# Two heads at a time on halves of the TensorE array in a hybrid attention layer

## Chip, cores and metric

One core of one Trainium2 chip runs the whole program. The metric is the device time of one execution in microseconds (us); the median of three runs is given. The engines are TensorE (PE; its weight loads are listed apart as PEld), VectorE (DVE), ScalarE (ACT), GpSimd (POOL) and SyncE (SP), which here issues every DMA.

## What is computed

Two layers over 512 frames of width 1024, all in float32. Each layer projects the normalised input, runs three groups of heads side by side (head width 64), projects their outputs back, and applies a squared-ReLU feed-forward of width 4096. Cut to what matters:

```python
z = rms(x, norm1) @ w_in
ya = swa(...)      # A: 8 query heads, 2 kv heads, window of whole 64-frame chunks, sinks
yb = fox(...)      # B: 4 heads, blocks of 128 queries
#   s = q @ k.T / 8 + F[q] - F[k]; causal; p = softmax(s); o = p @ v
yc = mlstm(...)    # C: 4 heads; scores Sm = (q @ k.T) * exp(Dm - m) per block, plus a running state
x = x + concat([ya, yb, yc]) @ w_out
x = x + square(relu(rms(x, norm2) @ w_ff1)) @ w_ff2
```

## The kernel before

Every large weight matmul is done as three matmuls on parts of float32 numbers (`mm3`, lines 306 to 308: high times high, high times low, low times high). ACT rounds a weight tile to its high part (line 201), DVE subtracts to get the low part (line 202). These weight matmuls are called W below; one over 512 columns in the output projection follows the next by about 0.23 us.

The attention stage of a layer interleaves W with the small matmuls of the three head groups. `fill(us)` puts W into the program until a credit of that many microseconds is used up; generators `runA`, `runB` and `runC` put small steps between. PE, DVE and ACT each work through their own queue in order; a scheduler has set that order when the program is built, mostly along the order of the code. `att()` hands out one of eight PSUM banks of 128x512.

A small float32 matmul is two matmul instructions in the trace (two passes), so counts in the profile are twice those of the code; the transposes through `ident` are one. Shapes such as `64*128` tell how many rows and columns of the 128x128 array the instruction uses: all small matmuls are full (`128*128`) except these:

- A, scores (line 763): `64*128`, the two kv heads `r` lie in the two row halves. Values (line 819): `128*64`, `r` picks the column half. A chunk from the third on has further keys, whose value product (line 822) is full and is added to the same bank.
- B, scores (line 864): `64*128`, head `2*pr + r` lies in row half `r`; a causal mask is added by a bf16 matmul (line 866, full). Values (line 900): `128*64`, into column half `r` of the bank `pobs[pr]`.
- C, scores (line 964): `64*128`.

In `runB` a unit is a head and a block `n` of 128 queries, 16 units a layer, with `nk = (n+1)*128` keys. Step s1 does the scores and the softmax: DVE adds the row of F and takes the maximum (line 869), negates it (871), ACT takes the exponential and its sum (873), DVE divides (875, 876). s2 transposes the probabilities (885) and copies them out of PSUM (888 on ACT, 890 on DVE). s3 multiplies by the values (900). `runC` makes a decay table E per head (line 951, from a row that a DMA spreads over the partitions, `rowb`), multiplies the scores into it (965), forms numerator and denominator (976 to 992), normalises (995 to 997), gates on POOL (1001), and transposes back (1008). The lines that close a layer's attention stage:

```python
        fill_to("wo0")     # output projection, inputs from A
        c_tail(0)          # transposes of heads 0, 1 of C
        fill(3.0, "wo1")   # output projection, inputs from B (yg tiles 4 and 5)
        c_tail(1)          # transposes of heads 2, 3 of C
        fill_to("wo1")
```

Of the kernel before, what the change touches and what calls it, by code (L numbers as in the profile page):

```python
# [25 lines left out]
NT = S // P  # L26
NCH = S // 64
# [18 lines left out]
def trunk(ctx, tc, x, cols, rows, gate_w, tabs, w_in, w_out, w1, w2, out):  # L46
    nc = tc.nc
    V, A, G, T = nc.vector, nc.scalar, nc.gpsimd, nc.tensor
# [11 lines left out]
    def nm(s):  # L60
        cnt[0] += 1
        return f"{s}_{cnt[0]}"

    ATT = {"ms": (S, 5), "zq": (640, 6), "zv": (260, 8), "tmp": (768, 3), "rowb": (S, 2),
           "qk": (2 * S, 5), "pT": (S, 4), "hs": (256, 2), "co": (256, 4)}
    FFP = {"xbx": (8 * D, 1), "fraw": (S, 9), "fs": (S, 6), "ct": (S, 6), "ms": (S, 2)}
    phase = {}
# [242 lines left out]
    ident = cst.tile([P, P], F32, name="ident")  # L310
# [97 lines left out]
    identb = cst.tile([P, P], BF16, name="identb")  # L408
    trib = cst.tile([P, P], BF16, name="trib")
# [29 lines left out]
    def rowb(drow, r):  # L439
        b = wt("rowb", "rowb")  # L440
        nc.sync.dma_start(b, drow[r:r + 1, :].broadcast_to((P, S)))
        return b
# [29 lines left out]
            rope.append((Cg, Sg))  # L472
        LPS[l].update(sk=sk, onorm=onorm, gb=gb, rope=rope)

    FA, FB = 1.4, 0.21
    F0, F1, F2 = 0, 4.5, 1.5
    FG = 4
    for l in range(L):
# [25 lines left out]
        gate = {}  # L504
# [43 lines left out]
        done = set()  # L548
# [199 lines left out]
        def runA():  # L748
# [5 lines left out]
            st = {}  # L754
# [57 lines left out]
            def s3(c):  # L812
                t, odd = divmod(c, 2)
                w, vt, p1, p2 = st.pop(c)
                po = att()
                for g in range(2):
                    for r in range(2):
                        u = 2 * g + r
                        T.matmul(po[r * 64:(r + 1) * 64, g * P:(g + 1) * P], vt[:w, r * 64:(r + 1) * 64],  # L819
                                 p1[:w, u * P:(u + 1) * P], start=True, stop=p2 is None)  # L820
                    if p2 is not None:
                        T.matmul(po[:, g * P:(g + 1) * P], vbd[:, c % 4], p2[:, g * P:(g + 1) * P],  # L822
                                 start=False, stop=True)
                cols = slice(c * 64, (c + 1) * 64)
                A.activation(yg[:, 0:4, cols], v3(po[:, :256]), AF.Copy)
                V.tensor_tensor(yg[:, 8:12, cols], v3(po[:, :256]), yg[:, 0:4, cols], ALU.subtract)

            for i in range(NCH + 2):
                if i < NCH:
                    s1(i)  # L830
                yield
                if 0 <= i - 1 < NCH:
                    s2(i - 1)
                yield
                if 0 <= i - 2 < NCH:
                    s3(i - 2)
                yield

        qTB, kTB, qTC, kTC = [None] * 4
# [11 lines left out]
                             scale=gfox(l, i))  # L851

        def runB(qTB, kTB):
            units = [(h, n) for h in range(4) for n in range(NT)]
            st, pobs, fbs = {}, {}, {}

            def s1(u):
                h, n = units[u]
                pr, r = divmod(h, 2)
                if n == 0:  # L860
                    fbs[h] = rowb(gate["drow"], h)
                nk = (n + 1) * P
                sp = att()
                T.matmul(sp[:, :nk], qTB[r * 64:(r + 1) * 64, pr, n * P:(n + 1) * P],  # L864
                         kTB[r * 64:(r + 1) * 64, pr, :nk], start=True, stop=False)
                T.matmul(sp[:, n * P:nk], identb, trib, start=False, stop=True)  # L866
                scs = wt("ms", "scs")
                mx = smt(1, "mxb")
                V.tensor_tensor_reduce(scs[:, :nk], sp[:, :nk], fbs[h][:, :nk], 1.0, -3.0e38, ALU.add, ALU.max, mx)
                nmx = smt(1, "nmxb")  # L870
                V.tensor_scalar(nmx, mx, -1.0, None, ALU.mult)
                ssum = smt(1, "ssb")
                A.activation(scs[:, :nk], scs[:, :nk], AF.Exp, bias=nmx, accum_out=ssum)
                rec = smt(1, "recb")
                V.reciprocal(rec, ssum)
                V.tensor_scalar(scs[:, :nk], scs[:, :nk], rec, None, ALU.mult)
                st[u] = scs

            def s2(u):
                h, n = units[u]  # L880
                nk = (n + 1) * P
                scs = st.pop(u)
                pt = att()
                for b in range(n + 1):
                    T.transpose(pt[:, b * P:(b + 1) * P], scs[:, b * P:(b + 1) * P], ident)  # L885
                p_ = wt("pT", "pTb")
                if n % 2:
                    A.activation(p_[:, :nk], pt[:, :nk], AF.Copy)
                else:
                    V.tensor_copy(p_[:, :nk], pt[:, :nk])  # L890
                st[u] = p_

            def s3(u):
                h, n = units[u]
                pr, r = divmod(h, 2)
                if r == 0 and n == 0:
                    pobs[pr] = att()
                p_ = st.pop(u)
                for b in range(n + 1):
                    T.matmul(pobs[pr][r * 64:(r + 1) * 64, n * P:(n + 1) * P], zbv[b][:, h * 64:(h + 1) * 64],  # L900
                             p_[:, b * P:(b + 1) * P], start=b == 0, stop=b == n)
                if r == 1 and n == NT - 1:
                    A.activation(yhi(4 + pr), pobs[pr], AF.Copy)
                    V.tensor_tensor(ylo(4 + pr), pobs[pr], yhi(4 + pr), ALU.subtract)

            for i in range(len(units) + 2):
                if i < len(units):
                    s1(i)
                yield
                if 0 <= i - 1 < len(units):  # L910
                    s2(i - 1)
                yield
                if 0 <= i - 2 < len(units):
                    s3(i - 2)
                yield

        def prepC(t, qTC, kTC):
# [23 lines left out]
        def runC(qTC, kTC, C):  # L941
# [13 lines left out]
                                fill=0.0, base=0, channel_multiplier=-1)  # L955
                es[h] = e

            def s1(h):
                pr, r = divmod(h, 2)
                rs = slice(r * 64, (r + 1) * 64)  # L960
                sp = att()
                for sb in range(NT):
                    cs_ = slice(sb * P, (sb + 1) * P)
                    T.matmul(sp[:, cs_], kTC[rs, pr, cs_], qTC[rs, pr, cs_], start=True, stop=True)  # L964
                V.tensor_tensor(es[h], sp, es[h], ALU.mult)
                yield

            def s2(h):
# [43 lines left out]
            def run():  # L1012
                for i in range(4 + 2):
                    if i < 4:
                        yield from s0(i)
                    yield
                    if 0 <= i - 1 < 4:
                        yield from s1(i - 1)
                    yield
                    if 0 <= i - 2 < 4:  # L1020
                        yield from s2(i - 2)
# [30 lines left out]
        for _ in runA():  # L1052
            fill(FA, "co")
            step += 1
            if step in (4, 7):
                next(g2_, None)
            if "bk" in done and step >= 9 and step % 2 == 0 and bt < 2 * NT:
# [6 lines left out]
        ct = 0  # L1064
        gb = runB(qTB, kTB)
        qTC, kTC = qk2("qTC"), qk2("kTC")
        cst_ = wt("qk", "state")[:, :780].rearrange("p (b r v) -> p b r v", b=3, r=2)
        G.memset(cst_, 0.0)
        for i in range(8):
            next(gb)  # L1070
# [9 lines left out]
        while live:  # L1080
            for g_ in list(live):
                if next(g_, "end") == "end":
                    live.remove(g_)
                fill(FB, "wo0")
        fill_to("wo0")
        c_tail(0)
        fill(3.0, "wo1")
# [216 lines left out]
```

## Time and profile before

| | |
|---|---|
| median of 3 runs | 1168.75 us (1167.68 to 1170.32) |
| span of the profiled execution, first to last instruction | 1168.6 us |
| PE busy | 1161.6 us, 99% |
| DVE busy | 856.5 us, 73% |
| ACT busy | 590.7 us, 51% |
| POOL busy | 60.8 us, 5% |
| granted TensorE clock, mean | 0.998 |

The page gives the span alone for the profiled execution; it lies 0.15 us below the median of the runs, so a sum against the span is a sum against the time. Layer 0's group A runs from 83.1 us (first line 763) to 156.1 us (first line 864), its groups B and C from there to 227.1 us (the second block of line 1008); layer 1's from 660 to 805 us in the same pattern. Matmuls overlap their neighbours in the trace, so that the distance from one start to the next tells what one costs, and not its listed duration.

### The profile page before, as it was taken

What the parts mean: (1) busy time and instruction counts of PE and PEld (TensorE: products, weight loads), DVE (VectorE), ACT (ScalarE), POOL (GpSimd) and SP (SyncE); (2) the same over time, 40 slices, a digit from 0 to 9 for tenths busy, and PEclk for the clock granted to TensorE, in tenths of its full rate; (3) what the DMA queues carried; (4) which work ended last, traced back from release to release, by engine and by line L of the source; (5) the groups of instructions that cost most, each with busy time, mean ns of one, the idle gap of its engine ahead of it and who ended that gap; (6) DMA issues with size and microseconds to landing.
All of it is one profiled execution on the core that took longest, in us unless ns stands there. A gap on an engine that the chain in (4) does not pass through costs nothing.

```text
span 1168.6 us, 19784 instructions
## 1 busy us (share of the span) xinstructions
PE 1161.6 (99%) x7348; PEld 1012.7 (87%) x7348; DVE 856.5 (73%) x1803; ACT 590.7 (51%) x1249; POOL 60.8 (5%) x98
## 2 busy tenths in 40 slices
PE   8999999999999999999999999999999999999998
PEld 8999877787899989889899988777788898998887
DVE  7686766798587687676867776777975776786684
ACT  5445654365454454455444465634645554554551
POOL 2020011103000000000001100110000000000000
PEclk9999999999999999999999999999999999999999
DMA  6332122243242332321333321214232233232221
GB/s 219 117 91 64 55 77 68 80 141 105 73 123 84 96 114 82 118 63 47 116 92 99 92 63 56 69 54 149 91 96 86 91 107 105 87 121 88 64 73 72
DMA packets 60000, 107.69 MB, mean 92 GB/s; under 512 B 7152, under 2 KB 8560, under 8 KB 59904
## 3 DMA queue, kind: packets, MB, share of 16 engines
q1 hardware_dynamic: 59904, 106.43, 29.5%
q8 instruction: 58, 0.95, 0.3%
q14 instruction: 38, 0.31, 0.1%
HBM read 103.82 MB, written 2.13 MB: 91 GB/s over the span
## 4 chain that ended last, share of the span: by engine, by line
PE 98%; DMA 1%; SPq 0%; DVE 0%; issue 0%; ACT 0%; ACTq 0%
PE at L306 29%; PE at L307 28%; PE at L308 28%; PE at L864 2%; PE at L900 2%; PE at L763 1%; PE at L819 1%; PE at L822 1%; PE at L885 1%; PE at L964 1%; PE at L796 1%; PE at L982 1%; DMA prm<-in_rows_dram 0%; DMA xT<-in_x_dram 0%; PE at L866 0%; DMA raw<-in_w_in_dram 0%
## 5 line engine op out<-in xcount | busy, mean ns | idle before, releaser
L201 ACT ACTIVATE whi<-raw 128x512 fp32r<-128x512 f32 x264 | 167.0, 633 | 217.8 <-PE at L307 155.2
L306 PE MATMUL at<-yg,whi 128*128 128x512 f32 (+1 forms) x644 | 255.5, 398 | 0.0
L307 PE MATMUL at<-yg,whi 128*128 128x512 f32 (+1 forms) x644 | 253.0, 393 | 0.0
L308 PE MATMUL at<-yg,wlo 128*128 128x512 f32 (+1 forms) x644 | 252.9, 393 | 0.0
L202 DVE TENSOR_TENSOR wlo<-raw,whi 128x512 fp32r<-128x512 f32 x264 | 180.2, 688 | 83.4 <-ACT whi L201 78.5
L306 PE MATMUL at<-whi,xh 128*128 128x256 f32 (+1 forms) x640 | 187.4, 293 | 1.3 <-ACT whi L201 1.3
L307 PE MATMUL at<-wlo,xh 128*128 128x256 f32 (+1 forms) x640 | 181.9, 284 | 0.1
L308 PE MATMUL at<-whi,xl 128*128 128x256 f32 (+1 forms) x640 | 181.8, 284 | 0.0
L308 PEld LDWEIGHTS at<-yg,wlo 128*128 128x128 f32 x644 | 121.0, 188 | 28.3
L306 PEld LDWEIGHTS at<-yg,whi 128*128 128x128 f32 x644 | 121.2, 188 | 24.0 <-issue 0.7
L307 PEld LDWEIGHTS at<-yg,whi 128*128 128x128 f32 x644 | 121.2, 188 | 24.1 <-issue 0.7
L306 PE MATMUL at<-xh,whi 128*128 128x256 f32 (+1 forms) x416 | 131.9, 317 | 0.0
L307 PE MATMUL at<-xl,whi 128*128 128x256 f32 (+1 forms) x416 | 131.3, 316 | 0.0
L308 PE MATMUL at<-xh,wlo 128*128 128x256 f32 (+1 forms) x416 | 131.1, 315 | 0.0
L306 PEld LDWEIGHTS at<-whi,xh 128*128 128x128 f32 x640 | 122.4, 191 | 5.5 <-issue 3.4
L307 PEld LDWEIGHTS at<-wlo,xh 128*128 128x128 f32 x640 | 122.2, 191 | 0.5 <-DVE wlo L202 0.4
L308 PEld LDWEIGHTS at<-whi,xl 128*128 128x128 f32 x640 | 122.3, 191 | 0.0
L201 ACT ACTIVATE whi<-fraw 128x512 fp32r<-128x512 f32 x96 | 60.8, 633 | 101.5 <-PE at L307 101.5
L307 PE MATMUL at<-xbx,whi 128*128 128x256 f32 x384 | 108.0, 281 | 0.0
L306 PE MATMUL at<-xbx,whi 128*128 128x256 f32 x384 | 107.9, 281 | 0.0
L308 PE MATMUL at<-xbx,wlo 128*128 128x256 f32 x384 | 107.8, 281 | 0.0
L202 DVE TENSOR_TENSOR wlo<-fraw,whi 128x512 fp32r<-128x512 f32 x96 | 65.0, 688 | 47.1 <-ACT whi L201 42.8
(268 smaller groups left out, 1931.9 us busy)
## 6 DMA issues: line engine op xcount, KB each, us to landing
raw<-in_w_dram SPq DMA_DIRECT2D x160, 256.0 KB, 2.6
fraw<-in_w_dram SPq DMA_DIRECT2D x96, 256.0 KB, 2.7
raw<-in_w_in_dram SPq DMA_DIRECT2D x80, 256.0 KB, 2.7
raw<-in_w_out_dram SPq DMA_DIRECT2D x32, 256.0 KB, 2.6
rowb<-drow SPq DMA_DIRECT2D x16, 256.0 KB, 3.4
xT<-in_x_dram SPq DMA_DIRECT2D x8, 256.0 KB, 4.5
out_dram<-xT SPq DMA_DIRECT2D x7, 256.0 KB, 2.1
cssn<-in_tabs_dram SPq DMA_DIRECT2D x2, 256.0 KB
```

What stands on the lines that cost most here:

```text
L201: A.activation(hi[:, :512], src, AF.Copy)
L202: V.tensor_tensor(lo[:, :512], src, hi[:, :512], ALU.subtract)
L306: T.matmul(o, sh, mh, start=first, stop=False)
L307: T.matmul(o, sh, ml, start=False, stop=False)
L308: T.matmul(o, sl, mh, start=False, stop=last)
L763: T.matmul(sc[r][:, g * 256:g * 256 + nk], qTA[g][r * 64:(r + 1) * 64, c * P:(c + 1) * P], kTA[r * 64:(r + 1) * 64, k0:k0 + nk], start=Tru ...
L796: T.transpose(pt[:w, u * P:(u + 1) * P], pe[:, u, :w], ident)
L819: T.matmul(po[r * 64:(r + 1) * 64, g * P:(g + 1) * P], vt[:w, r * 64:(r + 1) * 64], p1[:w, u * P:(u + 1) * P], start=True, stop=p2 is None)
L822: T.matmul(po[:, g * P:(g + 1) * P], vbd[:, c % 4], p2[:, g * P:(g + 1) * P], start=False, stop=True)
L864: T.matmul(sp[:, :nk], qTB[r * 64:(r + 1) * 64, pr, n * P:(n + 1) * P], kTB[r * 64:(r + 1) * 64, pr, :nk], start=True, stop=False)
L885: T.transpose(pt[:, b * P:(b + 1) * P], scs[:, b * P:(b + 1) * P], ident)
L900: T.matmul(pobs[pr][r * 64:(r + 1) * 64, n * P:(n + 1) * P], zbv[b][:, h * 64:(h + 1) * 64], p_[:, b * P:(b + 1) * P], start=b == 0, stop= ...
```

## The change

1. A's s3: the four value matmuls of a chunk stand together, then the two full ones; s3 stands right behind s1 of a later chunk, and a chunk has two `fill` steps and not three. `FA` goes from 1.4 to 2.1.
2. B: a unit is a pair of heads and a block, 8 units a layer. The scores of both heads stand next to each other, in the two row halves, then the two masks; the value matmuls alternate between the column halves. Negation and reciprocal are done once for both heads (128x2). Copies of the probabilities go to DVE for the even head and to ACT for the odd one. s3 follows s1. The scores have a buffer tag of their own (`scs`, 4), apart from `ms`; `rowb` has 4 buffers and not 2.
3. C: the scores of two heads alternate between the row halves, after the decay tables of both.
4. The steps of B, C and W are dealt out anew; `FB` goes from 0.21 to 0.33. 2 KB a partition are set aside for DMAs that software describes, which gives room for the buffers.

```diff
-    ATT = {"ms": (S, 5), ..., "rowb": (S, 2),
+    ATT = {"ms": (S, 5), ..., "rowb": (S, 4), "scs": (S, 4),
-    FA, FB = 1.4, 0.21
+    FA, FB = 2.1, 0.33
 # runA, s3
-                for g in range(2):
-                    for r in range(2):
-                        u = 2 * g + r
-                        T.matmul(po[r*64:(r+1)*64, g*P:(g+1)*P], vt[:w, ...], p1[:w, ...], start=True, stop=p2 is None)
-                    if p2 is not None:
-                        T.matmul(po[:, g*P:(g+1)*P], vbd[:, c % 4], p2[:, ...], start=False, stop=True)
+                for u in range(4):
+                    g, r = divmod(u, 2)
+                    T.matmul(po[r*64:(r+1)*64, g*P:(g+1)*P], vt[:w, ...], p1[:w, ...], start=g == 0, ...)
+                if p2 is not None:
+                    for g in range(2):
+                        T.matmul(po[:, g*P:(g+1)*P], vbd[:, c % 4], p2[:, ...], start=False, stop=True, ...)
 # runA and runB, the loop over units
                 s1(i)
+                s3(i - 2)
                 yield
                 s2(i - 1)
                 yield
-                s3(i - 2)
-                yield
 # runB
-            units = [(h, n) for h in range(4) for n in range(NT)]
+            units = [(pr, n) for pr in range(2) for n in range(NT)]
+                sps = [att(), att()]
+                for r, sp in enumerate(sps):
+                    T.matmul(sp[:, :nk], qTB[rs, pr, n*P:(n+1)*P], kTB[rs, pr, :nk], start=True, stop=False)
+                for sp in sps:
+                    T.matmul(sp[:, n*P:nk], identb, trib, start=False, stop=True)
...
+                for b in range(n + 1):
+                    for r in range(2):
+                        T.matmul(pobs[pr][r*64:(r+1)*64, n*P:(n+1)*P], zbv[b][:, ...], ps[r][:, b*P:(b+1)*P], ...)
 # runC, s1
-            def s1(h):
+            def s1(pr):
+                sps = [att(), att()]
                 for sb in range(NT):
-                    T.matmul(sp[:, cs_], kTC[rs, pr, cs_], qTC[rs, pr, cs_], start=True, stop=True)
+                    for r, sp in enumerate(sps):
+                        T.matmul(sp[:, cs_], kTC[rs, pr, cs_], qTC[rs, pr, cs_], start=True, stop=True)
 # driver of B and C
-        live = [gc, gb]
-        while live: ...
+        for _ in gc:
+            ct += 1
+            fill(FB, "wo0")
+            if 5 * bt < 2 * ct:
+                bt += 1
+                next(gb, None)
+                fill(FB, "wo0")
+        for _ in gb:
+            fill(FB, "wo0")
```

In the changed file the lines have moved: 819 is 818, 864 to 866 keep their numbers, 885 is 889, 900 is 906, 903 is 909, 964 is 969, 982 is 988, 1001 is 1007, 1008 is 1014.

How PE's queue stands at a chunk of group A, layer 0, before (`zar`, `vsh` and `kva` hold values, `pT` probabilities, `z` rows of B that are transposed):

```order
L848 MATMUL at_1687<-ident,z_848 128x128 x4
L819 MATMUL at_1694<-pT_1554,zar_503 64x128 x2
L822 MATMUL at_1694<-pT_1559,kva_674 128x128
L819 MATMUL at_1694<-pT_1554,zar_503 64x128 x2
L822 MATMUL at_1694<-pT_1559,kva_674 128x128
L306 MATMUL at_1474<-whi_1353,xh 128x256
```

The same place after, with the scores of a later chunk in front:

```order
L763 MATMUL at_1737<-kva_674,qTA_672 128x192
L763 MATMUL at_1738<-kva_674,qTA_672 128x192
L763 MATMUL at_1737<-kva_674,qTA_673 128x192
L763 MATMUL at_1738<-kva_674,qTA_673 128x192
L818 MATMUL at_1764<-pT_1694,vsh_1196 64x128 x4
L822 MATMUL at_1764<-pT_1699,kva_674 128x128 x2
```

Half-array and full matmuls of the values alternated twice; now the four half ones are one block, behind the half-array scores.

PE's queue in groups B and C, layer 0, before: the scores of a unit with `n` = 2 behind the values of a unit with `n` = 3 (`kTB`, `qTB` are keys and queries, `zbv` values, `pTb` transposed probabilities, `scs` scores):

```order
L964 MATMUL at_2508<-qTC_2236,kTC_2237 128x128 x4
L900 MATMUL at_2395<-pTb_2466,zbv_1241 64x128
L900 MATMUL at_2395<-pTb_2466,zbv_1243 64x128
L900 MATMUL at_2395<-pTb_2466,zbv_1245 64x128
L900 MATMUL at_2395<-pTb_2466,zbv_1247 64x128
L864 MATMUL at_2518<-kTB_1195,qTB_1194 128x384
L866 LDWEIGHTS identb
L866 MATMUL at_2518<-trib,identb 128x128
L885 MATMUL at_2533<-ident,scs_2479 128x128 x2
```

And after, a unit with `n` = 3 and the values of one with `n` = 1:

```order
L864 MATMUL at_2472<-kTB_1195,qTB_1194 128x512
L864 MATMUL at_2473<-kTB_1195,qTB_1194 128x512
L866 LDWEIGHTS identb
L866 MATMUL at_2472<-trib,identb 128x128
L866 LDWEIGHTS identb
L866 MATMUL at_2473<-trib,identb 128x128
L906 MATMUL at_2429<-pTb_2448,zbv_1241 64x128
L906 MATMUL at_2429<-pTb_2453,zbv_1241 64x128
L906 MATMUL at_2429<-pTb_2448,zbv_1243 64x128
L906 MATMUL at_2429<-pTb_2453,zbv_1243 64x128
L889 MATMUL at_2501<-ident,scs_2415 128x128 x3
L889 MATMUL at_2507<-ident,scs_2416 128x128 x3
```

Neighbouring half-array matmuls now go to different halves; before, all of a block went to the same one.

ACT's queue at the end of the stage, before (`hsq`, `rhl`, `rhy` belong to the normalisation of C's last head, line 903 copies B's output to `yg`):

```order
L888 ACTIVATE pTb_3020<-at_3015 128x512
L420 ACTIVATE rhl_2987<-rhv_2985 128x4
L1009 ACTIVATE yg<-at_3039 128x512
L422 ACTIVATE rhy_2989<-rhl_2987 128x4
L903 ACTIVATE yg<-at_2739 128x512
L201 ACTIVATE whi_3070<-raw_2574 128x512
```

And after:

```order
L892 ACTIVATE pTb_2925<-at_2920 128x512
L432 ACTIVATE hsq_2971<-hs_2969 128x256
L909 ACTIVATE yg<-at_2728 128x512
L420 ACTIVATE rhl_2977<-rhv_2975 128x4
L422 ACTIVATE rhy_2979<-rhl_2977 128x4
L201 ACTIVATE whi_3022<-raw_2556 128x512
L1015 ACTIVATE yg<-at_3034 128x512
```

The normalisation of C's last head stood ahead of the copy of B's output, and now stands behind it.

More of the change, by code (lines that the diff above doesn't have):

```diff
@@ L62, in nm @@
         return f"{s}_{cnt[0]}"
-    ATT = {"ms": (S, 5), "zq": (640, 6), "zv": (260, 8), "tmp": (768, 3), "rowb": (S, 2),
+    ATT = {"ms": (S, 5), "zq": (640, 6), "zv": (260, 8), "tmp": (768, 3), "rowb": (S, 4), "scs": (S, 4),
            "qk": (2 * S, 5), "pT": (S, 4), "hs": (256, 2), "co": (256, 4)}
@@ L830, in runA @@
                     s1(i)
+                if 0 <= i - 2 < NCH:
+                    s3(i - 2)
                 yield
@@ L853, in runB @@
         def runB(qTB, kTB):
-            units = [(h, n) for h in range(4) for n in range(NT)]
+            units = [(pr, n) for pr in range(2) for n in range(NT)]
             st, pobs, fbs = {}, {}, {}
             def s1(u):
-                h, n = units[u]
-                pr, r = divmod(h, 2)
+                pr, n = units[u]
                 if n == 0:
-                    fbs[h] = rowb(gate["drow"], h)
+                    fbs[pr] = [rowb(gate["drow"], 2 * pr + r) for r in range(2)]
                 nk = (n + 1) * P
[L863 to L870, printed above, removed]
+                sps = [att(), att()]
+                for r, sp in enumerate(sps):
+                    rs = slice(r * 64, (r + 1) * 64)
+                    T.matmul(sp[:, :nk], qTB[rs, pr, n * P:(n + 1) * P], kTB[rs, pr, :nk], start=True, stop=False)
+                for sp in sps:
+                    T.matmul(sp[:, n * P:nk], identb, trib, start=False, stop=True)
+                scs = [wt("scs", "scs") for _ in range(2)]
+                mx, nmx, ssum, rec = (smt(2, n_) for n_ in ("mxb", "nmxb", "ssb", "recb"))
+                for r, sp in enumerate(sps):
+                    V.tensor_tensor_reduce(scs[r][:, :nk], sp[:, :nk], fbs[pr][r][:, :nk], 1.0, -3.0e38, ALU.add,
+                                           ALU.max, mx[:, r:r + 1])
@@ L871, in s1 @@
                 V.tensor_scalar(nmx, mx, -1.0, None, ALU.mult)
-                ssum = smt(1, "ssb")
-                A.activation(scs[:, :nk], scs[:, :nk], AF.Exp, bias=nmx, accum_out=ssum)
-                rec = smt(1, "recb")
+                for r in range(2):
+                    A.activation(scs[r][:, :nk], scs[r][:, :nk], AF.Exp, bias=nmx[:, r:r + 1],
+                                 accum_out=ssum[:, r:r + 1])
                 V.reciprocal(rec, ssum)
-                V.tensor_scalar(scs[:, :nk], scs[:, :nk], rec, None, ALU.mult)
+                for r in range(2):
+                    V.tensor_scalar(scs[r][:, :nk], scs[r][:, :nk], rec[:, r:r + 1], None, ALU.mult)
@@ L877, in s1 @@
                 st[u] = scs
             def s2(u):
-                h, n = units[u]
+                pr, n = units[u]
                 nk = (n + 1) * P
                 scs = st.pop(u)
-                pt = att()
-                for b in range(n + 1):
[L885 to L902, printed above, removed]
+                ps = []
@@ new lines, in s2 @@
+                for r in range(2):
+                    pt = att()
+                    for b in range(n + 1):
+                        T.transpose(pt[:, b * P:(b + 1) * P], scs[r][:, b * P:(b + 1) * P], ident)
+                    p_ = wt("pT", "pTb")
+                    if r:
+                        A.activation(p_[:, :nk], pt[:, :nk], AF.Copy)
+                    else:
+                        V.tensor_copy(p_[:, :nk], pt[:, :nk])
+                    ps.append(p_)
+                st[u] = ps
@@ new lines, in s3 @@
+            def s3(u):
+                pr, n = units[u]
+                if n == 0:
+                    pobs[pr] = att()
+                ps = st.pop(u)
+                for b in range(n + 1):
+                    for r in range(2):
+                        h = 2 * pr + r
+                        T.matmul(pobs[pr][r * 64:(r + 1) * 64, n * P:(n + 1) * P], zbv[b][:, h * 64:(h + 1) * 64],
+                                 ps[r][:, b * P:(b + 1) * P], start=b == 0, stop=b == n)
+                if n == NT - 1:
@@ L908, in runB @@
                     s1(i)
+                if 0 <= i - 2 < len(units):
+                    s3(i - 2)
                 yield
@@ L1016, in run @@
                     yield
-                    if 0 <= i - 1 < 4:
-                        yield from s1(i - 1)
+                    if i in (2, 4):
+                        yield from s1(i // 2 - 1)
                     yield
@@ L1054, in trunk @@
             step += 1
-            if step in (4, 7):
+            if step in (3, 5):
                 next(g2_, None)
-            if "bk" in done and step >= 9 and step % 2 == 0 and bt < 2 * NT:
+            if "bk" in done and step >= 7 and bt < 2 * NT:
                 next(pb_)
@@ L1063, in trunk @@
         fill_to("co")
-        ct = 0
         gb = runB(qTB, kTB)
@@ L1069, in trunk @@
         for i in range(8):
-            next(gb)
+            if i % 2 == 0:
+                next(gb)
             fill(FB, "wo0")
@@ L1078, in trunk @@
         gc, c_tail = runC(qTC, kTC, cst_)
-        live = [gc, gb]
[L1080 to L1083, printed above, removed]
+        ct, bt = 0, 0
+        for _ in gc:
[4 more added lines that the diff above has]
+                next(gb, None)
                 fill(FB, "wo0")
+        for _ in gb:
+            fill(FB, "wo0")
         fill_to("wo0")
```

20 lines of the change are left out of this document (8 added, 12 removed).

## Prediction

> **What bounds the kernel now.** I read the page's first part, then the waits of PE, then PE's timeline in the two stages that change.
>
> ```profile
> span 1168.6 us, 19784 instructions
> PE 1161.6 (99%) x7348; PEld 1012.7 (87%) x7348; DVE 856.5 (73%) x1803; ACT 590.7 (51%) x1249; POOL 60.8 (5%) x98
> PE at L306 <- ACT whi L201: 1.3, 1, 1.3
> PE at L332 <- DVE zc L315: 1.1, 1, 1.1
> PE at L489 <- DVE accs L360: 1.0, 1, 1.0
> ```
>
> PE is busy all the time, and in the whole program it waits 3.4 us for another engine. So the time is the sum of PE's own steps, and a microsecond taken out of its queue is a microsecond of time, as long as what PE reads next is ready earlier too.
>
> What a half-array step costs is the distance of starts (first column, us). In group A, scores of four matmuls that alternate between the row halves (x8, two passes each), then W:
>
> ```profile
> 126.37 0.92 PE L763 MATMUL at<-kva,qTA 64*128 64x192 f32 x8
> 127.22 0.39 PE L306 MATMUL at<-whi,xh 128*128 128x256 f32 x1
> 127.45 0.28 PE L307 MATMUL at<-wlo,xh 128*128 128x256 f32 x1
> ```
>
> And a chunk's values, two matmuls in the two column halves (x4), then a full one, twice:
>
> ```profile
> 122.94 0.44 PE L819 MATMUL at<-pT,vsh 128*64 128x128 f32 x4
> 123.31 0.49 PE L822 MATMUL at<-pT,kva 128*128 128x128 f32 x2
> 123.73 0.44 PE L819 MATMUL at<-pT,vsh 128*64 128x128 f32 x4
> ...
> 124.34 0.37 PE L306 MATMUL at<-whi,xh 128*128 128x256 f32 x1
> ```
>
> Against these, blocks of groups B and C whose matmuls all go to one half:
>
> ```profile
> 169.48 0.48 PE L864 MATMUL at<-kTB,qTB 64*128 64x128 f32 x2
> 169.90 0.23 PE L866 MATMUL at<-trib,identb 128*128 128x128 bf16 x1
> ...
> 188.47 0.87 PE L900 MATMUL at<-pTb,zbv 128*64 128x128 f32 x6
> 189.27 0.70 PE L864 MATMUL at<-kTB,qTB 64*128 64x256 f32 x2
> 189.90 0.23 PE L866 MATMUL at<-trib,identb 128*128 128x128 bf16 x1
> ...
> 191.01 0.40 PE L307 MATMUL at<-yg,whi 128*128 128x512 f32 x1
> 191.25 0.40 PE L308 MATMUL at<-yg,wlo 128*128 128x512 f32 x1
> 191.58 1.09 PE L900 MATMUL at<-pTb,zbv 128*64 128x128 f32 x8
> 192.59 0.91 PE L864 MATMUL at<-kTB,qTB 64*128 64x384 f32 x2
> 193.44 0.23 PE L866 MATMUL at<-trib,identb 128*128 128x128 bf16 x1
> 193.47 0.48 PE L306 MATMUL at<-yg,whi 128*128 128x512 f32 x1
> 193.79 0.40 PE L307 MATMUL at<-yg,whi 128*128 128x512 f32 x1
> ...
> 196.20 1.16 PE L964 MATMUL at<-qTC,kTC 64*128 64x128 f32 x8
> 197.29 0.43 PE L900 MATMUL at<-pTb,zbv 128*64 128x128 f32 x2
> 197.65 1.12 PE L864 MATMUL at<-kTB,qTB 64*128 64x512 f32 x2
> 198.71 0.23 PE L866 MATMUL at<-trib,identb 128*128 128x128 bf16 x1
> ```
>
> From these come three prices. *One half*: L900 takes 0.80 us for three matmuls and 1.01 for four, so 0.21 each; L864 takes 0.42, 0.63, 0.85, 1.06 for 128 to 512 columns, so 0.21 for each 128 columns plus 0.21. *Both halves*: the 192 columns of L763 would cost 0.32 each at that rate, 1.28 for four, and the whole block takes 0.85, which is two times 0.32 and 0.21. L819's two matmuls would cost 0.43, and take 0.37 with all that goes with a block. So two halves run side by side at full rate, in rows and in columns. *A change between full, row-half and column-half use*: the step ahead of L900 takes 0.33 where the one before took 0.24, L900 x8 takes 0.16 over its four 0.21, and the first W behind a mask takes 0.32, again 0.09 more than usual. In and out are 0.09 + 0.16 + 0.09 = 0.34 to 0.35, about 0.18 a change.
>
> **The change, part by part (one layer).**
>
> *B's scores.* Eight pairs for sixteen single blocks: the passes of a head are 0.21 x (1+2+3+4) = 2.1 us, two heads' worth goes: 4.2. *B's values:* ten matmuls of 0.21 a head, again two heads of four go: 4.2. *C's scores:* 1.09 a head less 0.21 for its changes is 0.88; two of four go: 1.8. Together 10.2. The masks (L866) and transposes (L885) stay as many, as full matmuls.
>
> *Fewer changes in B and C.* Counted in PE's order from the first L864 to the second L1008, the kind of use changes 59 times before and 34 times after: 25 x 0.18 = 4.5.
>
> *A.* The values of a chunk go from two half blocks to one and stand directly behind half-array scores; counted from the first L763 to the first L864 the changes go from 46 to 28: 18 x 0.18 = 3.2. The passes stay, since L819 was already paired.
>
> Sum: 17.9 a layer, 35.8 for two.
>
> *What PE then waits for.* The cover shrinks, the work of the others hardly: DVE saves eight negations and eight reciprocals a layer (a row below), ACT nothing. In two halves of layer 0's B and C (columns: PE, PEld, DVE, ACT, POOL busy with counts, clock, DMA):
>
> ```profile
> 156.00:188.00 32.00, 31.99 (x180) 22.62 (x179) 24.92 (x88) 19.74 (x61) 5.38 (x7) 1.00 0.27 81
> 188.00:220.00 32.00, 32.00 (x177) 22.25 (x176) 24.33 (x90) 13.29 (x40) 4.91 (x13) 1.00 0.13 42
> ```
>
> PE's 32 us become about 25, and DVE has 24.9 in the first. It will be nearly full there, and PE must sometimes wait for a division (L878) or a copy of probabilities (L894). Lower end: nothing, since DVE may run ahead while PE does W. Upper end: 7 us a layer, if DVE reaches its work only at today's pace. I take 1, near the low end, since even after the cut the busy time fits into PE's.
>
> At the end of the stage there is a wait that I can place. After the last L906 the next four W (L306) read B's output, which ACT must copy first; the order shows the two small ACT steps of C's last head behind that copy, and then come three small DVE steps, one of 128x256 and four on POOL, before L1014 can run. The likes of these (form, busy us, mean ns):
>
> ```profile
> L903 ACT ACTIVATE yg<-at 128x512 fp32r<-128x512 f32 x2 | 1.2, 599 | 1.9 <-PE at L900 1.9
> L422 ACT ACTIVATE rhy<-rhl 128x4 f32<-128x4 f32 x4 | 0.8, 198 | 0.0
> L427 DVE SCALAR_TENSOR_TENSOR rhr<-rht,rhy 128x4 f32<-128x4 f32 x4 | 0.6, 156 | 0.0
> L997 DVE TENSOR_TENSOR hs<-hs,rhr 128x256 f32<-128x256 f32 x4 | 1.7, 420 | 0.0
> L1001 POOL TENSOR_TENSOR yt<-hs,co 128x64 f32<-128x64 f32 x16 | 5.4, 367 | 25.9 <-DVE nmxb L871 10.9 <-DVE den L991 8.7 <-DVE hs L997 6.3
> ```
>
> 0.6 + 2 x 0.2 + 3 x 0.16 + 0.42 + 4 x 0.34 (5.4/16) = 3.3 us. Between the last L906 and L1014 PE has eight W of 0.23, 1.9 us. The wait is nothing if the chain has run earlier after all, 1.4 as it stands, 3.3 if nothing covers it; I take 2, for the chain has seven hand-overs that these durations leave out.
>
> *Costs taken as nothing.* Row DMAs (`rowb`): with four buffers seven of eight are issued during A, and three of the four E tables are made there; they are hidden by A's W, and if ACT ran late the first to wait would be A's values. The larger `fill` steps deal out the same W. The smaller set-aside memory serves no DMA here, all being issued by SP.
>
> So 35.8 - 2 x (1 + 2) = 29.8, and 1168.6 - 29.8 = 1138.8: I say 1138. The median of the runs lies 0.15 above the span, which changes nothing.
>
> One rule speaks against two halves at full rate in a block of only two matmuls. The Trainium skill, "TensorE: Matmul & The Clock Gate", Part 3 (The mechanism), says that matmuls start and end strictly in program order; each head has two passes, so by that rule the second head's first pass could not start before the first head's second. L819's two matmuls speak against it: three passes of 0.107 and 0.16 to 0.2 for the block would be 0.48 to 0.52, two are 0.37 to 0.41, and 0.37 was measured. It stays as a rival below.
>
> **The rivals.**
>
> *DVE becomes the bound of B and C.* The softmax of a pair of full units needs, from L864 to L889:
>
> ```profile
> L869 DVE CUSTOM_DVE_ANT_0 scs<-at,rowb 128x512 f32<-128x512 f32 x4 | 2.7, 687 | 2.3 <-PE at L866 2.3
> L871 DVE TENSOR_SCALAR nmxb<-mxb 128x1 f32<-128x1 f32 x16 | 2.3, 147 | 0.1
> L873 ACT ACTIVATE scs<-scs,nmxb 128x512 f32<-128x512 f32 x4 | 2.9, 720 | 4.4 <-DVE nmxb L871 4.4
> L875 DVE RECIPROCAL recb<-ssb 128x1 f32<-128x1 f32 x16 | 2.6, 162 | 3.0 <-ACT scs L873 3.0
> L876 DVE TENSOR_SCALAR scs<-scs,recb 128x512 f32<-128x512 f32 x4 | 2.0, 510 | 0.0
> ```
>
> 1.4 + 0.15 + 1.4 + 0.2 + 1.0 = 4.2 us, through a queue shared with W's low parts (L202) and C. If DVE gets through the first half only at today's pace, PE waits the 7 us there that it has gained: 17.9 - 7 - 2 = 8.9 a layer, 1168.6 - 17.8 = 1150.8. For it: DVE's 24.9. Against: today it idles 7 of 32 us and PE never waits. The page "TensorEngine Tiling (Array Packing)" of the Trainium skill, section PSUM Bottleneck, states this rule: tiling speeds up the array but not the reading of PSUM, which may become the bound. No row before shows PE waiting for it.
>
> *The new pairs overlap in part, or not at all.* If a block takes one pass more than half of its passes (the second head starts one pass late), B's scores give back half of their 4.2, that is 2.1, and the eight blocks of values and two of C's scores 0.107 each, 1.1: 17.9 - 3.2 - 3 = 11.7 a layer, 1145. With no overlap only the changes are saved, 7.7 less the end's 2, and the time is 1157. For it: no row shows a pair over 512 columns. Against: L763 and L819.
>
> *Slower.* Each of the 16 pair units stalls PE at L889 or L906: at 35.8/16 = 2.2 us a unit the gain is gone, at 3 us it is 1181. It needs DVE's queue to put more than 5 us in front of the 4.2 us chain, against some 6 us of PE work (W, L906, L889, the next L864) between L864 and its L889. Today's queue has idle time, so this is unlikely.
>
> **How the numbers follow.** My forecast (pairs at full rate, waits of a few us) 0.62; without any wait it would be 1132.8. DVE as the bound 0.2, up to 1151. Pairs that overlap in part 0.09 (1145), not at all 0.04 (1157). Slower 0.03, no change 0.02. The range from 1131 to 1151 leaves out the last three, 0.09, and what lies below or between, some 0.1 more; its lower end takes the changes at 0.2 each and no waits (17.9 + 0.9 a layer: 1131). About 0.2% (2.3 us) is what a measurement can tell from no change; faster than that holds 0.95.
>
> **What would show it.** In the changed profile: L864 of 512 columns, x4, about 1.06 us ahead of L866; L906 x16 about 1.0; L969 x16 about 1.1; a block of L818 and L822 about 1.05 instead of 1.40; PE waits of 1 to 3 us a layer, for `yg` (L909) and `yt` (L1007); DVE's busy share in B and C well above today's 77% (49.25 of 64). The prediction is wrong if the pairs of L864 start a pass apart, or if PE's waits on `scs` or `pTb` exceed 5 us a layer.

## The result, and the profile after

The changed kernel takes 1138.44 us (median of four runs, 1137.52 to 1139.73), the kernel before 1169.05 beside it: 0.974 of its time, 95% interval 0.9728 to 0.9752, a gain of 30.6 us where 29.8 were worked out. The profiled execution after took 1137.61 us with a span of 1135.9. The page of the changed kernel and its list of PE's waits, against those shown of before (the waits that stand there too are left out, and two short ones of 0.3 us for `wlo` and 0.2 for `xl` ahead of the first attention stage; the columns are us in total, times, longest us):

```profile
span 1135.9 us, 19685 instructions
PE 1127.3 (99%) x7348; PEld 994.9 (88%) x7348; DVE 855.3 (75%) x1771; ACT 589.7 (52%) x1249; POOL 55.7 (5%) x98
```

```profile
PE at L306 <- ACT yg L909: 1.4, 2, 0.7
...
PE at L889 <- DVE state L943: 0.4, 2, 0.2
```

PE still runs 7348 records and is still busy 99% of a shorter span: passes run side by side, none were taken out. In the attention stages two waits are new, `yg` and `state`, 0.9 us a layer together.

The stages show where the gain lies. The distances are of PE's starts: A from the first L763 to the first L864, B and C from there to the start of the second block of L1014 (before: L1008, at 226.95 us in layer 0), one value for each layer. "Work" is from layer 0's first L763 to the end of the last instruction on an engine, and "ahead" is from the first instruction on an engine, 0.3 us into the span, to that L763.

| kernel | ahead | A | B and C | work |
|---|---|---|---|---|
| before | 82.77 | 73.04, 73.04 | 70.84, 70.87 | 1082.82 |
| changed | 81.35 | 69.70, 69.70 | 58.47, 58.39 | 1051.52 |
| changed, profiled again | 79.68 | 69.70, 69.71 | 58.50, 58.39 | 1051.53 |

A fell by 3.34 us a layer, B and C by 12.4, 31.5 for both layers, and the rest of the work is 0.2 longer (pauses of 1.1 right behind the last mark, which come up at the end of the experiments, less four W, 0.9, that now stand inside B and C). The part ahead differs by 1.7 us between two profiles of one and the same kernel, while the work repeats within 0.01. So the experiments below are read by the work, and a difference of medians under 2 us is not read without it.

The blocks that the prediction named, in PE's timeline of the changed kernel (start, us, line, tiles, count of passes), first in A, then in B and C:

```profile
108.01 0.66 PE L818 MATMUL at<-pT,zar 128*64 128x128 f32 x8
108.60 0.71 PE L822 MATMUL at<-pT,kva 128*128 128x128 f32 x4
109.06 0.36 PE L306 MATMUL at<-whi,xh 128*128 128x256 f32 x1
...
188.51 0.39 PE L308 MATMUL at<-yg,wlo 128*128 128x512 f32 x1
188.83 1.13 PE L864 MATMUL at<-kTB,qTB 64*128 64x512 f32 x4
189.89 0.28 PE L866 MATMUL at<-trib,identb 128*128 128x128 bf16 x2
190.11 0.66 PE L906 MATMUL at<-pTb,zbv 128*64 128x128 f32 x8
190.69 0.87 PE L889 MATMUL at<-ident,scs 128*128 128x128 f32 x6
...
192.89 1.16 PE L969 MATMUL at<-qTC,kTC 64*128 64x128 f32 x16
193.98 0.94 PE L982 MATMUL at<-state,qTC 128*128 128x130 f32 x6
```

L864 with two heads of 512 columns takes 1.06 us from start to start, which is what one head took before; 16 passes of L969 take 1.09, as 8 did, and 16 of L906 1.02. Values and full products of a chunk in A take 1.05 instead of 1.40. All four are the numbers forecast.

### The profile page after: what moved, and what is told of

Its sections match the earlier page's. It is cut to its first block, busy times and chain, and to the rows that moved or that the text cites. A ratio compares the mean times of both kernels' runs of the same rounds, so it can differ in the third digit from the quotient of the medians.

```text
span 1135.9 us, 19685 instructions
## 1 busy us (share of the span) xinstructions
PE 1127.3 (99%) x7348; PEld 994.9 (88%) x7348; DVE 855.3 (75%) x1771; ACT 589.7 (52%) x1249; POOL 55.7 (5%) x98
## 4 chain that ended last, share of the span: by engine, by line
PE 96%; DMA 1%; ACT 1%; DVE 1%; issue 0%; SPq 0%
PE at L306 29%; PE at L307 29%; PE at L308 29%; PE at L763 1%; PE at L906 1%; PE at L864 1%; PE at L889 1%; PE at L818 1%; PE at L822 1%; PE at L796 1%; PE at L988 1%; DMA xT<-in_x_dram 1%; DMA raw<-in_w_in_dram 0%; DMA prm<-in_rows_dram 0%; PE at L969 0%; PE at L847 0%
## 5 line engine op out<-in xcount | busy, mean ns | idle before, releaser
L308 PE MATMUL at<-yg,wlo 128*128 128x512 f32 (+1 forms) x644 | 252.8, 392 | 0.0
L306 PE MATMUL at<-whi,xh 128*128 128x256 f32 (+1 forms) x640 | 185.0, 289 | 1.7 <-ACT whi L201 1.7
L308 PE MATMUL at<-whi,xl 128*128 128x256 f32 (+1 forms) x640 | 181.2, 283 | 0.2 <-DVE xl L365 0.2
L308 PEld LDWEIGHTS at<-yg,wlo 128*128 128x128 f32 x644 | 121.0, 188 | 28.3
L308 PE MATMUL at<-xh,wlo 128*128 128x256 f32 (+1 forms) x416 | 131.1, 315 | 0.0
L308 PEld LDWEIGHTS at<-whi,xl 128*128 128x128 f32 x640 | 121.4, 190 | 0.6 <-DVE xl L365 0.6
L308 PE MATMUL at<-xbx,wlo 128*128 128x256 f32 x384 | 107.8, 281 | 0.0
```

The lines of the kernel that those rows point to most:

```text
L306: T.matmul(o, sh, mh, start=first, stop=False)
L308: T.matmul(o, sl, mh, start=False, stop=last)
```

## The experiments

**The control and the bound.** The changed kernel once more, unedited:

> The changed kernel, once more, as the yardstick of the three others on the same chip. Its first profile had 1135.9 us of span, of which 81.65 lie ahead of layer 0's first attention stage, and the others profiled so far had 80.0 to 80.9 there, so by all theories 1137 to 1138.5 us, with 69.70 us in each stage A and 58.4 us from the first score of B to the second output group of C.

It took 1137.56 us (ratio 0.9732, 0.9715 to 0.9749), with both stages as before within 0.03. This is the yardstick for the runs below that were made beside it.

Then work for VectorE alone, in B's softmax:

```diff
                                            ALU.max, mx[:, r:r + 1])
+                for r in range(2):
+                    V.tensor_tensor(scs[r][:, :nk], scs[r][:, :nk], zrow[:, :nk], ALU.add)
```

> Two additions of zero by VectorE for each pair of heads and query block of B, behind the exponential's input, 16 a layer; at the durations of such rows about 6.4 us of VectorE work a layer, in a stage (B and C) of 58.4 us in which VectorE is busy about 50. My theory (TensorE is the bound, VectorE has slack except in the first 19 us, where it is busy 17.7 of 18.9): the four units that fall in those 19 us bring about 3.2 us of work against 1.2 us of room, so 1 to 2 us a layer come through, 2 to 5 us in all: 1140 to 1143. Rival, VectorE already sets the pace of B and C: nearly all of 6.4 a layer, 10 to 13 us in all, 1148 or more. Rival, VectorE's work is hidden anywhere: under 1 us, 1138 to 1139.

1140.07 us (0.9757, 0.974 to 0.9774), work 1054.93: +3.4 us, as expected, where DVE was busy 12.9 longer (868.2 us against 855.3). The windows (us, then PE, PEld, DVE, ACT, POOL busy with counts, clock, DMA), two of the changed kernel in B and C, and the first of this one:

```profile
151.35:170.20 18.85, 18.67 (x113) 13.30 (x112) 17.69 (x62) 12.76 (x41) 3.53 (x4) 1.00 0.21 68
...
183.10:209.83 26.73, 26.03 (x178) 19.74 (x177) 21.90 (x72) 11.24 (x33) 4.31 (x14) 1.00 0.14 41
```

```profile
150.07:168.90 18.83, 18.30 (x106) 12.62 (x106) 18.58 (x62) 12.11 (x39) 3.18 (x4) 1.00 0.17 52
```

DVE is at 94% in the first 19 us of the changed kernel and at 99% with the added work; later in the stage it has room (82% at its end). So three quarters of the added work is hidden, and of the 1.7 us a layer that come through, layer 0 shows 1.35 within the first 20 us. DVE is near to being the bound in that one stretch, and isn't it in B and C as a whole.

**What a change of use costs.** First A alone, with its values as before (two short blocks for each chunk instead of one):

```diff
-                for u in range(4):
-                    g, r = divmod(u, 2)
-                    T.matmul(po[...], vt[...], p1[...], start=g == 0, stop=p2 is None, ...)
-                if p2 is not None:
-                    for g in range(2):
+                for g in range(2):
+                    for r in range(2):
+                        u = 2 * g + r
+                        T.matmul(po[...], vt[...], p1[...], start=True, stop=p2 is None)
+                    if p2 is not None:
...
```

> Group A's value matmuls in the order of before (two half, one full, twice), the rest as changed. My sum: 12 changes of use more a layer (38 instead of 26 in A), no passes: 12 x 0.18 x 2 = +4.3 us, 1142.7 us. If A's gain came from the dealing out of W and not from changes of use: no change, 1138.4.

1140.62 us (0.9765, 0.9748 to 0.9781). The median says only +2.2; the work says 1055.65, +4.1, and stage A 71.78 instead of 69.70: 2.08 us a layer for 12 changes, 0.173 each, against 0.18 taken. The block, where the changed kernel's above has 1.05 us:

```profile
107.11 0.44 PE L819 MATMUL at<-pT,zar 128*64 128x128 f32 x4
107.48 0.49 PE L822 MATMUL at<-pT,kva 128*128 128x128 f32 x2
107.90 0.44 PE L819 MATMUL at<-pT,zar 128*64 128x128 f32 x4
108.27 0.49 PE L822 MATMUL at<-pT,kva 128*128 128x128 f32 x2
108.51 0.36 PE L306 MATMUL at<-whi,xh 128*128 128x256 f32 x1
```

Same passes, 1.40 us. The price of a change to columns and back is right.

Then B's scores undone as a pair: the full-array mask between the two heads keeps their halves apart.

```diff
                     T.matmul(sp[:, :nk], qTB[rs, pr, n * P:(n + 1) * P], kTB[rs, pr, :nk], start=True, stop=False)
-                for sp in sps:
                     T.matmul(sp[:, n * P:nk], identb, trib, start=False, stop=True)
```

> The mask of each head stands right behind its scores, so that a full matmul lies between the two half-array ones. My sum (pairs run side by side only as neighbours, 0.18 us a change of use): B's scores cost 4.2 us a layer more, and 16 changes more (49 instead of 33) 2.9: 1138.4 + 14.2 = 1152.6 us. If PE in truth waits for DVE in B and C, part of this disappears in the waits: under 1145. If the gain of the pair does not come from running side by side: 1138.4 + 5.8 = 1144 (changes alone).

1146.98 us (0.9823, 0.9808 to 0.9838), work 1061.95: +10.4 where I expected 14.2. PE's timeline:

```profile
192.44 1.12 PE L864 MATMUL at<-kTB,qTB 64*128 64x512 f32 x2
193.49 0.23 PE L865 MATMUL at<-trib,identb 128*128 128x128 bf16 x1
193.65 1.12 PE L864 MATMUL at<-kTB,qTB 64*128 64x512 f32 x2
```

The heads run one after the other, 1.21 us from one's start to the next's. Over the stage, the starts behind scores and masks grew by 6.1 us a layer. Changes alone could be 16 x 0.17 = 2.7 of that; the rest is passes that no longer share the array. So the expectation from the changes alone (1144) falls, and that from DVE (below 1145) too. About half of what is missing to 7.1 is a pair that did not overlap in the changed kernel either (0.55, below). And some was given back: the order of the stage's end moved with the edit, and `yg` is not waited for there (0.7 a layer).

A change of use taken out, by writing the mask first, so that scores and values of neighbouring units stand side by side:

```diff
+                for sp in sps:
+                    T.matmul(sp[:, n * P:nk], identb, trib, start=True, stop=False, skip_group_check=True)
                 for r, sp in enumerate(sps):
                     rs = slice(r * 64, (r + 1) * 64)
-                    T.matmul(sp[:, :nk], ..., start=True, stop=False)
-                for sp in sps:
-                    T.matmul(sp[:, n * P:nk], identb, trib, start=False, stop=True)
+                    T.matmul(sp[:, :nk], ..., start=False, stop=True, skip_group_check=True)
```

> The causal mask is written into the score tiles ahead of the two heads' scores, which add to it, so that scores (rows) and value products (columns) stand side by side in five of the eight pair units of a layer: 29 changes between matmul forms instead of 33. As in the kernel with the mask between the heads, the end of the stage then reads: one projection matmul, the second-but-last output group, 24 projection matmuls, the last output group. If a change from row pairs to column pairs costs like the others, 4 changes are -0.7 us a layer; if it costs nothing, nearer -1.4. The waits for B's last copy (0.7) and for the input of the last output group (0.55) go: -1.25 a layer. In all -3.9 us (to -5.3), 1132.5 to 1134 beside 1137.6. Rival: the earlier mask makes the score tile be taken earlier, and TensorE waits for it at each unit: 0 to +2 us.

1136.67 us (0.9725, 0.9711 to 0.9738), but work 1051.49: nothing gained, a miss. In PE's timeline and waits:

```profile
187.44 0.40 PE L308 MATMUL at<-yg,wlo 128*128 128x512 f32 x1
187.68 0.29 PE L863 MATMUL at<-trib,identb 128*128 128x128 bf16 x2
187.90 1.13 PE L866 MATMUL at<-kTB,qTB 64*128 64x512 f32 x4
188.96 0.66 PE L907 MATMUL at<-pTb,zbv 128*64 128x128 f32 x8
189.55 0.87 PE L890 MATMUL at<-ident,scs 128*128 128x128 f32 x6
```

```profile
PE at L989 <- DVE E L972: 1.8, 2, 0.9
```

From L308 to the transposes it is 2.11 us, against 2.18 (188.51 to 190.69) in the changed kernel: the change taken out was worth 0.07, not 0.17. So the average price holds for in and out together, not for each step. Of the two waits at the stage's end only `yg` went (0.7 a layer): the last L1015 block still takes 0.84 us where it takes 0.36 without a wait. A new wait of 0.9 a layer for C's table `E` takes what was saved; why `E` comes late there I have not traced.

**Order of the passes.** Values with all of one head's products ahead of the other's:

```diff
-                for b in range(n + 1):
-                    for r in range(2):
+                for r in range(2):
+                    for b in range(n + 1):
```

> B's value matmuls stand head by head in a block, all of the even head, then all of the odd one; no change of use is added. If matmuls start in the order of the queue, only the last of the one and the first of the other overlap: 4.2 us a layer less 8 x 0.11, so +6.7 to +8.4: 1145 to 1147 us. If each half has a queue of its own that looks past its neighbour: no change, 1138.4. If DVE or ACT is the bound: under +3.

1139.92 us (0.9762, 0.9748 to 0.9777), work 1054.47: +1.5 a layer. Two theories of the expectation fall: strict order would cost more than twice that, and free look-ahead nothing. The time would fit the third, a bound by DVE or ACT (under +3), but the loss lies in PE's own blocks: those below are 7, 269 and 487 ns longer, 1.5 us for the two pairs of a layer. The starts of single passes in the trace tell why. Here A is the first head's pass, B the second's, ns from the block's start; the order of the instructions is all A, then all B, two passes to a matmul. (The trace doesn't name the half of a pass. I tell them apart by time: each block falls into two series of equal number, and within a series the starts lie 0.11 us apart or more.)

```
 4 A, 4 B:  A 0  B 13   A 161  B 173 ...                           block 595, changed kernel 588
 6 A, 6 B:  A 0  A 160  A 269  B 275  A 378 ...                    block 1075, changed kernel 806
 8 A, 8 B:  A 0  A 160  A 269  A 378  A 488  B 493  A 597 ...      block 1512, changed kernel 1025
```

The second head's first pass starts with A's first, third and fifth: each time when three A passes ahead of it in the order have not started. It overtakes them, in the other half of the array, and in these blocks never more than three. C's scores by head show the same in the profile itself:

```diff
-                for sb in range(NT):
-                    for r, sp in enumerate(sps):
+                for r, sp in enumerate(sps):
+                    for sb in range(NT):
```

> C's scores of a pair stand head by head in one block instead of alternating. My sum: two blocks a layer give up 0.88 us each, less one pass of 0.11: +3.1 to +3.5 us, 1141.5 to 1142 us. With queues of their own for the halves: no change.

```profile
175.16 1.38 PE L969 MATMUL at<-qTC,kTC 64*128 64x128 f32 x13
176.27 0.48 PE L864 MATMUL at<-kTB,qTB 64*128 64x256 f32 x1
176.38 0.38 PE L969 MATMUL at<-qTC,kTC 64*128 64x128 f32 x2
176.59 0.38 PE L864 MATMUL at<-kTB,qTB 64*128 64x256 f32 x1
176.60 0.27 PE L969 MATMUL at<-qTC,kTC 64*128 64x128 f32 x1
```

In PE's order all sixteen passes of L969 stand ahead of L864. In the trace L864, in the free half, starts ahead of the last three. The time was 1139.93 (0.9759, 0.9744 to 0.9773), work 1054.56, +1.5 a layer: 1.0 from the scores, the rest in the stage's end, whose order moved too and where `yt` is waited for 1.2. The rule weighed in the prediction, from the Trainium skill, "TensorE: Matmul & The Clock Gate", Part 3 (The mechanism), that matmuls start strictly in program order, does not hold in these rows. Nor does PE work through its queue strictly in order, as the section on the kernel before has it: passes of the two halves can start out of order.

The reading can be put to a test: in twos (four passes of one head, then four of the other) nothing should be lost.

```diff
+                for b, r in [(b, r) for g in range(0, n + 1, 2) for r in range(2)
+                             for b in range(g, min(g + 2, n + 1))]:      # values; C's scores alike
```

> Value products of B and scores of C in twos: two matmuls (four passes) of one head, then two of the other, the order of everything else as in the changed kernel. My theory, from the blocks of the two kernels by head (the other half's first pass began as soon as it was the fourth after the running one): nothing is lost, within 0.2 us a layer of the changed kernel, 1137 to 1138.2. Rival, strict order of the passes: each group of two waits for the one ahead, so 12 and 16 passes lose a third to a half of their gain: 2 to 3 us a layer, 1142 or more. Rival, two in a row already cost part: 0.3 to 0.8 us a layer.

1138.17 us (0.9737, 0.9724 to 0.9751), work 1052.10: +0.3 a layer, a little over my 0.2 and where the last rival begins (0.3 to 0.8). The blocks themselves lose 0.2 of it, B's values 0.1, against the 1.5 of the order by head, and C's scores 0.1, against 1.0. So groups of four passes lose little, but not nothing. Strict order (2 to 3 us a layer) falls.

**Waits at the end of the stage.** Three orders. B's values ahead of the next scores (`s3(i - 2)` put in front of `s1(i)`):

> In a step of B the value products stand ahead of the next pair's scores instead of behind them. TensorE's order then has 29 instead of 33 changes between matmul forms in B and C of a layer, and 8 projection matmuls between the last values and C's second output group. If a change costs what stage A showed (2.08 us for 12, 0.17 each): 4 fewer are -0.7 us a layer; the wait for the last values' copy before the projection (0.7) goes too, the one pair whose scores are now parted by values gives back up to 0.4: -1 us a layer, -2 in all, 1135.5 to 1137. If the score's result now comes later to VectorE, which is busy 94% in the first 19 us, that costs 0.5 to 1.5 us a layer: 1138 to 1140.

1138.99 us (0.9744, 0.9729 to 0.9758), work 1053.41: +0.9 a layer, a miss, on the side of the rival. `yg` is still waited for, and 0.55 for `E` and 0.25 for `pTb` came on top, a layer.

B's steps earlier:

```diff
-            if 5 * bt < 2 * ct:
+            if 2 * bt < ct:
```

> B's steps advance at one for every two steps of C (before: two for five), so that B ends earlier and 24 projection matmuls (5.6 us) stand between C's two output groups; the number of changes is 34 instead of 33 a layer. My theory: the two waits at the end of the stage, for the copy of B's last values (0.7 us a layer) and for the input of the second output group (0.55), go, and one change is added (0.17): -1.1 us a layer, -2.2 in all, 1135 to 1136.5. Rival: the waits move with B's end, into the middle of C, where VectorE then is late for the denser scores: 0 to +2 us.

1148.41 us (0.9824, 0.9808 to 0.984), work 1062.01: +5.2 a layer, far outside both. PE's timeline at the end of the stage, and a window right behind the wait (the column behind POOL is the clock):

```profile
212.87 0.40 PE L308 MATMUL at<-yg,wlo 128*128 128x512 f32 x1
216.31 1.31 PE L1014 MATMUL at<-ident,yt 128*128 128x128 f32 x4 [3.04 <-POOL yt L1007]
217.26 0.78 PE L306 MATMUL at<-yg,whi 128*128 128x512 f32 x1
217.84 0.63 PE L307 MATMUL at<-yg,whi 128*128 128x512 f32 x1
218.27 0.63 PE L308 MATMUL at<-yg,wlo 128*128 128x512 f32 x1
218.69 0.63 PE L306 MATMUL at<-yg,whi 128*128 128x512 f32 x1
219.12 0.50 PE L307 MATMUL at<-yg,whi 128*128 128x512 f32 x1
219.46 0.40 PE L308 MATMUL at<-yg,wlo 128*128 128x512 f32 x1
```

```profile
216.31:219.19 2.88, 2.88 (x9) 2.21 (x10) 0.69 (x1) 0.60 (x1) 0.77 (x3) 0.50 0.39 119
```

C's last head now ends alone, its chain of small steps behind other DVE work, and 24 W are not enough cover: 3.04 us of waiting. And the granted clock is 0.50 for 2.9 us behind it: the five W behind L1014 take 2.20 us instead of 1.24, another 1.0. (L1014 itself takes 0.95, hardly more than its 0.92 in the changed kernel: there too its four transposes start 0.28 us apart, as POOL's four steps of `yt` end.) The wait (3.0), the clock (1.0) and L889 and L906 blocks that are 1.8 longer, of which 0.6 are waits for `pTb`, less 0.7 for `yg` make 5.1 of the 5.2.

Last, only more W ahead of the last output group:

```diff
-        fill(3.0, "wo1")
+        fill(5.6, "wo1")
```

> The end of the stage alone: 30 instead of 20 projection matmuls between C's two output groups (the planner is asked for 5.6 us instead of 3.0). The wait for the input of the last group (0.55 us a layer) goes, the wait for B's last copy (0.7) stays: -1.1 us in all, about 1136.5. If the waiting is only moved to the projection that needs the last group's output: no change, 1137.6.

1135.91 us (0.9715, 0.9702 to 0.9729), work 1048.92: 2.6 less, more than twice what I expected, since both waits went. The changed kernel's end, and this one's:

```profile
202.67 0.60 PE L1014 MATMUL at<-ident,yt 128*128 128x128 f32 x4
203.03 0.48 PE L306 MATMUL at<-yg,whi 128*128 128x512 f32 x1
...
205.98 1.09 PE L906 MATMUL at<-pTb,zbv 128*64 128x128 f32 x16
207.77 1.19 PE L306 MATMUL at<-yg,whi 128*128 128x512 f32 x4 [0.70 <-ACT yg L909]
...
209.83 1.16 PE L1014 MATMUL at<-ident,yt 128*128 128x128 f32 x4
210.75 0.48 PE L307 MATMUL at<-yg,whi 128*128 128x512 f32 x1
```

```profile
206.32 1.09 PE L906 MATMUL at<-pTb,zbv 128*64 128x128 f32 x16
207.35 0.50 PE L307 MATMUL at<-yg,whi 128*128 128x512 f32 x1
...
211.40 0.60 PE L1014 MATMUL at<-ident,yt 128*128 128x128 f32 x4
211.76 0.48 PE L306 MATMUL at<-yg,whi 128*128 128x512 f32 x1
```

In the changed kernel the second L1014 block takes 0.92 us where the first takes 0.36: 0.56 of waiting for `yt`, in three short pauses behind POOL's steps that the list of waits does not name, besides 0.70 for `yg`. With the longer fill other W, whose inputs are ready, follow L906 at once, and L1014 takes 0.36. This version has the shortest work of all: 2.6 us less than the changed kernel, 0.25%. The medians alone do not show that, as their intervals overlap.

## Why the prediction was right, step by step

- **Halves side by side.** Forecast at full rate; L864, L969 and L818 with L822 came at 1.06, 1.09 and 1.05 us as written. One of the eight pairs of L864 in a layer did start apart, which the prediction named as a sign of being wrong; under the waits it turns out to be a wait, not halves that fail to overlap.
- **Changes, A.** 3.2 forecast, 3.34 measured, and 12 of the 18 changes measured alone at 0.173. The reading that gave the 0.18 is less sound than its outcome: the rows run from W to L900, L864, the mask and W again, three changes and not one way in and out, and the 0.21 that L864 takes beyond its columns is left out, though for C's scores the same 0.21 is put down to changes. With it the stretch has 0.09 + 0.16 + 0.21 + 0.09 = 0.55 for three changes, which happens to be 0.18 again.
- **Changes and passes, B and C.** 14.7 forecast. The stage fell by 12.4, with two W (0.47 us) more in it and 1.45 us of waits (0.70, 0.2 and 0.55; the pauses for `yt` lie behind the stage's last mark): 14.3. By the distances of starts, without the waits, B's scores gave 5.9, B's values 5.5 and C's scores 2.25, where 4.2, 4.2 and 1.8 were forecast for their passes; the masks took 0.6 more, and the other steps gave 1.3. That does not part passes from changes within a block, and the mask-first run shows that the 0.18 is an average of unlike changes. (The 33 of the expectations are the 34 of the prediction without the step into the stage.)
- **Waits.** Taken as 2 at the end and 1 in the middle. At the end 0.70 + 0.56 = 1.3, in the places named, and nearer to the 1.4 of the prediction's own sum than to the 2 that it took. In the middle 0.2 at L889, and 0.55 here:

```profile
160.75 1.47 PE L864 MATMUL at<-kTB,qTB 64*128 64x384 f32 x4
162.15 0.28 PE L866 MATMUL at<-trib,identb 128*128 128x128 bf16 x2
...
183.08 0.92 PE L864 MATMUL at<-kTB,qTB 64*128 64x384 f32 x4
183.93 0.28 PE L866 MATMUL at<-trib,identb 128*128 128x128 bf16 x2
```

  The same pair takes 1.40 us at 160.75 and 0.85 at 183.08. The second head starts 0.59 us late there, as DVE's four `state` steps (L943), which read a score-sized PSUM tile, end; the load of its weights waits for a semaphore of DVE, and the last of these steps has just ended. That this tile is the one it needs I infer from the times. Waits were the step over-sized, 3.0 against 2.0 a layer. That is 2.0 us for both layers; A gave 0.3 more than forecast, B and C 0.7 less, and together these make the 1.5 or so between 29.8 and the 31.3 of the work.
- **The base.** I took the span of 1168.6 as the execution's time, and its nearness to the median as a reason. But a span leaves out about 1.7 us: the profiled execution after has that much around its span, and another run of the kernel before with a span of 1168.6 took 1170.29. Against that time the sum would have been 1140.5, and against the median of 1169.05 it is 1139.25. The sum itself gave 1138.8, of which 1138 was said. So part of the closeness to 1138.44 is luck: small errors that cancel, a base too low and a gain too small.
- **DVE as the bound**, a rival, was right in its sign and wrong in size: DVE is busy 86% in B and C (50.17 of 58.48 us) and 94% in the first 19 us, and PE waits 0.75 us a layer for it there, not 7. The added work shows that more would come through mostly in that stretch.
- **Overlap in part.** Not so: but for the one pair that waits, the two heads' first passes start 6 to 7 ns apart. In the order by head, a block loses more than a few ns only beyond four passes a head.

## What to carry to other kernels

Where one engine is busy all the time, price a block by the distance of its starts in the stage where it stands, and count changes between full and half use of the array in trips (in and out), since a single change taken out was worth only 0.07 us. Matmuls of two halves need not alternate one by one: four passes of one half standing together cost 0.2 us a layer here, six and eight cost 1.5 in B alone. Behind the gain look at the end of the stage for the chain that nothing covers any more; ten more independent matmuls a layer there were worth 2.6 us, while moving B's steps forward cost 10.5.

## What the runs showed of the hardware

- Matmuls of one array half overtake up to three passes of the other half that stand ahead of them and have not started: with 6 and 8 passes a head the second head began 275 and 493 ns into the block, with 4 at 13 ns, and L864 started ahead of the last three passes of L969.
- A wait of 3.04 us on PE was followed by a granted clock of 0.50 for 2.9 us, in layer 1 as in layer 0; waits of 0.7 us were not, as W ran at 0.23 us behind them.
- Time ahead of the first attention stage varied from 79.68 to 81.35 us in one kernel, while the 1051.5 us behind it agreed within 0.01.
